# A two-layer attention trunk: where the second layer's gate is summed, and when the first layer's h is transposed

## The chip, the cores and the metric

The kernel runs on one core of a Trainium2 chip. Its time is the device time of one execution in microseconds (us), the median of several executions. The core's engines each work through their own queue in order: TensorE (PE, matmuls and transposes), VectorE (DVE), ScalarE (ACT), GpSimd (POOL) and SyncE (SP, which issues most of the DMAs). They wait for each other by semaphores.

## The reference

Two layers, each with 256 tokens of width 1024, all in float32:

```
mod = silu(c) @ w_ada + b_ada                 # w_ada: 1024 x 3072 per layer
shift, scale, gate = split(mod, 3)
h   = rms_norm(x, norm_g) * (1 + scale) + shift
z   = h @ w_in        # [c_q | c_kv | k_rope | g_mla | q | k | v | g_moba]
o_A = MLA causal attention (8 heads)     o_B = block-sparse causal attention (8 heads)
y   = concat(silu(g_mla) * o_A, silu(g_moba) * o_B) @ w_out
x   = x + gate * y
```

`c` is one row, so `mod` is a product of a vector and a matrix: 3072 columns for each layer, of which shift, scale and gate have 1024 each. The gate is needed only at the end of its layer, where it multiplies y; shift and scale are needed at its start.

## The kernel before

Everything is unrolled once by a planner inside the program (`Clock`). Coroutines for loads, splits, attention and so on wait in a heap by planned times; TensorE's large products are "units" that `run` takes in a written order, and between two units it lets every coroutine go whose planned time has come. What a coroutine issues stands in its engine's queue from then on, in that order. `charge` adds planned costs, `idle` holds back an instruction while its engine's planned queue is full, and `warm` puts dummy products of the identity (tile `idle`) in where TensorE is planned to stand still for more than `GAP` (2 us); `DENSE` sets how many.

**Products.** A weight (`raw_*`) comes by DMA in pieces of 256 rows; ScalarE mostly makes its rounded fp32r half (`whi_*`) and VectorE the rest (`wlo_*`, `split_lo`). h has halves `h_hi` and `h_lo` too, and each product is three matmuls (`mm3`): hi by hi, hi by lo, lo by hi. z goes by groups: `za` (latents and rotary key), `zga` and `zgb` (gates of the heads), `zbq`, `zbk`, `zbv`; `q` and `kv` come from the latents, `s`, `ptr` and `oT` are attention, `y` the output product. `URGENT` says how near to its use a split is no longer held back by `idle`.

**Modulation.** `w_ada` is read through 5 buffers (`ada`), each two k-tiles of 128 rows by 512 columns. `on_tensor` visits a block of 512 columns once all 8 k-tiles are there: `groups_sum` multiplies each k-tile by `crep` (silu(c) repeated 32 times), in TensorE's 32-column form, four k-tiles at once in four groups of 32 output rows. A block of shift or scale is then copied to `ev`, transposed and added up (`ss_sums`). A block of the gate is copied to `evg` (`gate_rows`) and a product with `rowsel` adds up its four rows and spreads the sum to all partitions (`gate_sums`); VectorE adds `b_ada`. `on_vector` is the other way, not used before: VectorE multiplies a k-tile by silu(c) of its rows and adds it to `acc`, k after k, and a product with `ones` adds up the partitions.

`modulation(l)` covers the gate of layer l and, in layer 0, shift and scale of layer 1. Before, all goes `on_tensor`: eight visits of 512 columns, first both gate blocks of layer 0, then layer 1's four blocks of shift and scale, then both gate blocks of layer 1. `ada_loader` loads in the same order, and all loads share SP's queue with the weights. `PERIOD` holds the planned distance of pieces on VectorE, a delay, and the planned distance of pieces on TensorE.

**h.** Layer 0's shift and scale are summed in five rounds (`sum_first`), as `w_ada` comes in. `h_T` transposes the normalised x (`xr`) on TensorE into `htr`, multiplies by scale and adds shift there (`ss`), and makes `h_hi` and `h_lo`. It waits for `ss` before it issues the transposes. At the layer boundary the second token tile's x (t = 1) comes from the last `y`, and TensorE goes through `za` of the first tile, some `zbq` of the first tile, and then `za` of the second.

Of the kernel before, what the change touches and what calls it, by code (L numbers as in the profile page):

```python
# [23 lines left out]
DEPTH = 2  # L24
# [10 lines left out]
PS = 4  # L35
MARGIN = 0.0
GAP = 2.0
DENSE = 0.6
BQ_FIRST = 2
ON = ("T", "T")  # L40
EARLY = True
FIRST = 0
TOGETHER = 9
VISIT = 8
WAIT = 0.25
# [8 lines left out]
LAG = 3  # L54
AHEAD = 4
SLACK = 0.35
URGENT = 2
BIAS = 0.7
WARM = 7
D_LAT = 0.95  # L60
D_0 = 4.0
HALVES = 12
DUMMY = 12
PERIOD = ((4.0, 0.0, 7.0), (8.0, 0, 20.0))
C_A, W_A = 0, 416
C_GA, C_QB, C_KB, C_VB, C_GB = 416, 928, 1440, 1952, 2464

# [7 lines left out]
class Clock:  # L75
# [34 lines left out]
    def give(self, tag, n=1):  # L110
        self.free[tag].extend([self.end + self.LAT] * n)

    def take(self, tag, n=1, spare=0):
        f = self.free[tag]
        while len(f) < n + spare:
            yield lambda: len(f) >= n + spare
        f.sort()
        t = f[n - 1]
        del f[:n]
        yield t  # L120

    def until(self, *keys):
        if not all(k in self.done for k in keys):
            yield lambda: all(k in self.done for k in keys)
        yield max(self.done[k] for k in keys)
# [7 lines left out]
    def start(self, gen, at=None):  # L133
        self.push(self.end if at is None else at, gen)
# [73 lines left out]
    def warm(self, t):  # L208

        if self.dummy and t - self.t["T"] > GAP:  # L210
            self.now, self.end, self.engine = self.t["T"], self.t["T"], None
            self.dummy(int((t - self.t["T"]) * DENSE / 0.11))

# [58 lines left out]
def trunk(ctx, tc, x, c, positions, norm_g, w_ada, b_ada, w_in, mla_q_norm_g, mla_w_uq,  # L272
# [10 lines left out]
    clk = Clock()  # L283
    V, A, T = Metered(nc.vector, "V", clk), Metered(nc.scalar, "A", clk), Metered(nc.tensor, "T", clk)
    P, G = Metered(nc.gpsimd, "P", clk), nc.gpsimd
    done, take, give, until, start, run = clk.done, clk.take, clk.give, clk.until, clk.start, clk.run

    def bank(name):
        return pp.tile([128, 512], F32, tag="ps", bufs=8, name=name)
# [48 lines left out]
    ones = cp.tile([128, 128], F32, name="ones")  # L338
# [65 lines left out]
    vec_a = cp.tile([128, N_A], F32, name="vec_a")  # L404
# [148 lines left out]
    def splitter():  # L553
        for i, (key, a, src) in enumerate(pieces):
# [4 lines left out]
            yield from take("w")  # L559
            urgent = lambda: i <= used[0] + URGENT  # L560
            raw, tag = halves[key, a]
# [68 lines left out]
    def ss_finish(l, w, ks, p_):  # L630

        n = len(ks)
        o = ss[l][:, w * 8 + ks[0]:w * 8 + ks[0] + n]
        b0 = V_B + 16 * l + w * 8 + ks[0]
        V.tensor_tensor(o, p_, vec_a[:, b0:b0 + n], op=ALU.add)
        if w == 1:
            V.scalar_tensor_tensor(o, o, 1.0, vec_a[:, V_NG + 8 * l + ks[0]:V_NG + 8 * l + ks[0] + n],
                                   op0=ALU.add, op1=ALU.mult)
        clk.mark(*(("ss", l, w, k) for k in ks))
# [27 lines left out]
    def on_vector(todo, begin, period):  # L667

        for i, ((m, w, j), k) in enumerate(todo):
            yield begin + i * period  # L670
            c0 = w * D + j * 512
            yield from until(("ada", m, c0, k))
            if k == 0:
                yield from take("acc")
                acc = acc_tile(f"acc{m}{j}")
            for n in range(2):
                yield from clk.idle("V")
                s_ = ada[m, c0, k][:, n]
                if k + n == 0:
                    V.tensor_scalar(acc, s_, cs[:, 0:1], None, op0=ALU.mult)  # L680
                else:
                    V.scalar_tensor_tensor(acc, s_, cs[:, k + n:k + n + 1], acc, op0=ALU.mult, op1=ALU.add)
                clk.engine = None
            give("ada")
            if k == KT - 2:
                yield
                start(gate_sums(m, j, acc, ones), clk.now)

    def gate_rows(l, j, p_):
        yield from take("acc")  # L690
# [6 lines left out]
    def gate_sums(l, j, acc, sel_):  # L697

        yield from take("ps")
        p_ = bank(f"ada{l}2{j}")  # L700
        T.matmul(p_, lhsT=sel_, rhs=acc, start=True, stop=True)
        give("acc")
        yield
        yield from until(("bg", l))
        g_ = gate[l][:, j * 512:j * 512 + 512]
        V.tensor_tensor(g_, p_, g_, op=ALU.add)
        give("ps")
        clk.mark(("gate", l, 2 * j), ("gate", l, 2 * j + 1))
# [7 lines left out]
    ada = {}  # L716

    def modulation(l, period):

        by_k = lambda blocks: [(b, k) for b in blocks for k in range(0, KT, 2)]  # L720
        gates_ = by_k((l, 2, j) for j in range(2))
        next_ = by_k((l + 1, w, j) for j in range(2) for w in (1, 0)) if l + 1 < DEPTH else []
        start(ada_loader(l, (gates_ + next_)))
        if ON[l] == "V":
            yield clk.now + period[1]
            start(on_vector(gates_, clk.now, period[0]), clk.now)
        start(on_tensor((gates_ if ON[l] == "T" else []) + next_, clk.now + period[1], period[2]), clk.now)
        yield from take("gate")
        gate[l] = cp.tile([128, D], F32, tag="gate", bufs=1, name=f"gate{l}")
        load(gate[l], bass.AP(tensor=b_ada.tensor, offset=b_ada[l, 2 * D:].offset, ap=[[0, 128], [1, D]]), ("bg", l))  # L730

    def on_tensor(todo, begin, period):

        for i, ((m, w, j), k) in enumerate(todo):
            if (k + 2) % VISIT:
                continue
            c0 = w * D + j * 512
            ks = range(k + 2 - VISIT, k + 2, 2)
            yield from until(*(("ada", m, c0, b) for b in ks))
            if k + 2 == VISIT:  # L740
                yield from take("ps", spare=1)
                p_ = bank(f"ada{m}{w}{j}")
            key = ("visit", m, w, j, k)

            def emit():
                groups_sum(p_, [ada[m, c0, b][:, n] for b in ks for n in range(2)], ks[0])
                give("ada", len(ks))
                clk.mark(key)
            clk.offer(max(clk.now, done["ada", m, c0, k] + ADA_LAG), emit, begin + i * period)
            yield from until(key)  # L750
            if k == KT - 2:
                start(gate_rows(m, j, p_) if w == 2 else ss_sums(m, w, tuple(range(4 * j, 4 * j + 4)), p_), clk.now)

    def ada_loader(l, todo):
        if l:
            yield from until(("loaded", l - 1))
        for (m, w, j), k in todo:
            yield from load_ada(m, w * D + j * 512, k)
        clk.mark(("loaded", l))
# [23 lines left out]
    def h_T(xr, l, groups):  # L783

        ps_ = []
        if l or not FIRST:
            yield from until(*(("ss", l, w, k) for w in (1, 0) for ks, _ in groups for k in ks))
# [692 lines left out]
    for l in range(DEPTH):  # L1480
        L = Ls[l]
        if l == 0 or not EARLY:
            start(modulation(l, PERIOD[l]))
        todo = names[l]
        if l == 1:
            first = L.proj(todo[0])
            second, m = L.proj(todo[1]), 2 * BQ_FIRST
# [5 lines left out]
        for name in todo:  # L1493
            run(L.gates(name) if name in ("ga", "gb") else mix(L.proj(name)))
        if l == 0 and EARLY:
            start(modulation(1, PERIOD[1]))
# [42 lines left out]
```

## Time and profile before

| | |
|---|---|
| time, median of 3 executions | 310.87 us (310.55 to 311.05) |
| profiled execution, its own time | 309.71 us |
| its span, first to last instruction | 307.6 us |
| TensorE busy | 296.6 us (96%) |
| VectorE busy | 217.0 us (71%) |
| ScalarE busy | 211.0 us (69%) |
| TensorE's mean granted clock | 0.992 |
| DMA | 65.20 MB, mean 212 GB/s |

Matmuls overlap in the array, so a row's duration is longer than the distance to the next row's start; that distance is what a matmul costs. In a timeline a row ends with the idle time ahead of it and what ended it, in brackets. All vector, scalar and tensor instructions have the line of the helper that records them (L230), so they are told apart by their tiles.

### The profile page before, as it was taken

How to read it: one execution, taken by the hardware profiler on the slowest of the kernel's cores; microseconds unless marked ns; L12 is line 12 of the kernel's file. 1: busy time of each engine (PE TensorE's matmuls, PEld its weight loads, DVE VectorE, ACT ScalarE, POOL GpSimd, SP SyncE). 2: the span in 40 equal slices, each digit the busy share in tenths (PEclk: the TensorE clock that was granted, in tenths of full speed). 3: DMA queues.
4: the chain of work that ended last, by engine and by line, in shares of the span. 5: the costliest groups of instructions: out<-in, count | busy, mean ns of one | idle time of the engine just before them, and what ended most of it. 6: DMA issues, size and time to landing. Idle time of an engine off the chain costs nothing.

```text
span 307.6 us, 5595 instructions
## 1 busy us (share of the span) xinstructions
PE 296.6 (96%) x1976; PEld 234.7 (76%) x1976; DVE 217.0 (71%) x635; ACT 211.0 (69%) x516; POOL 13.6 (4%) x40
## 2 busy tenths in 40 slices
PE   6989999999999899999999998999999999999995
PEld 5757779986668588665775968879999778777884
DVE  1344798664997979784876778699877598857544
ACT  5443367796695886986678896877587959685710
POOL 8700000000010000000000000000000000000000
PEclk9799999999999999999999999999999999999998
DMA  7999996895979975781843976665606450621012
GB/s 237 315 351 355 362 372 193 275 389 204 359 212 376 329 256 172 255 286 25 320 120 122 336 258 215 200 168 175 205 12 208 128 174 32 207 78 57 3 65 71
DMA packets 40299, 65.20 MB, mean 212 GB/s; under 512 B 2685, under 2 KB 16325, under 8 KB 40272
## 3 DMA queue, kind: packets, MB, share of 16 engines
q1 hardware_dynamic: 39360, 63.71, 62.5%
q0 software_dynamic: 816, 1.12, 1.4%
q8 instruction: 15, 0.25, 0.3%
q14 instruction: 12, 0.10, 0.1%
q10 hardware_dynamic: 96, 0.02, 0.0%
HBM read 63.79 MB, written 1.06 MB: 211 GB/s over the span
## 4 chain that ended last, share of the span: by engine, by line
PE 81%; DVE 7%; DMA 5%; ACT 5%; issue 1%; SPq 0%
PE y L230 15%; PE zbv L230 7%; PE ada L230 7%; PE zgb L230 7%; PE zga L230 7%; PE zbq L230 6%; PE zbk L230 6%; PE s L230 6%; PE za L230 4%; PE oT L230 4%; DMA raw_bv<-in_w_in_dram 3%; PE ptr L230 3%; PE q L230 2%; PE qtr L230 2%; DMA ada<-in_w_ada_dram 2%; PE warm L230 1%
## 5 line engine op out<-in xcount | busy, mean ns | idle before, releaser
L230 ACT ACTIVATE P<-P,sm 128x128 f32<-128x128 f32 (+1 forms) x116 | 47.8, 446 | 6.7 <-DVE sm L230 6.6
L230 PE MATMUL ada<-ada,crep 128*32 128x512 f32 (+2 forms) x272 | 25.2, 471 | 1.5 <-DMA ada<-in_w_ada_dram 1.5
L230 PE MATMUL y<-whi_o,gm 128*128 128x512 f32 (+1 forms) x72 | 23.8, 386 | 0.5 <-DVE gm L230 0.5
L230 DVE TENSOR_TENSOR wlo_o<-raw_o,whi_o 128x1024 fp32r<-128x1024 f32 x16 | 19.5, 1222 | 3.8 <-ACT whi_o L230 3.8
L230 PE MATMUL zga<-h_hi,whi_ga 128*128 128x256 f32 x64 | 19.3, 302 | 0.0
L230 PE MATMUL zgb<-h_hi,whi_gb 128*128 128x256 f32 x64 | 19.2, 300 | 0.0
L230 PE MATMUL zga<-h_hi,wlo_ga 128*128 128x256 f32 x64 | 18.2, 285 | 0.7 <-DVE wlo_ga L230 0.7
L230 PE MATMUL zgb<-h_hi,wlo_gb 128*128 128x256 f32 x64 | 18.1, 283 | 0.0
L230 PE MATMUL zga<-h_lo,whi_ga 128*128 128x256 f32 x64 | 18.1, 283 | 0.0
L230 PE MATMUL zgb<-h_lo,whi_gb 128*128 128x256 f32 x64 | 18.1, 283 | 0.0
L230 ACT CAST whi_o<-raw_o 128x1024 fp32r<-128x1024 f32 x15 | 15.6, 1044 | 1.6 <-PE y L230 1.6
L230 PEld LDWEIGHTS y<-whi_o,gm 128*128 128x128 f32 x72 | 13.1, 189 | 3.4 <-DVE gm L230 0.9
L230 PE MATMUL ptr<-ident,P 128*128 128x128 f32 x96 | 15.6, 273 | 0.0
L230 ACT ACTIVATE htr<-htr,ss 128x128 f32<-128x128 f32 (+1 forms) x21 | 9.7, 473 | 8.4 <-PE htr L230 5.0
L230 PEld LDWEIGHTS ptr<-ident,P 128*128 128x128 f32 x96 | 12.1, 140 | 4.4 <-DVE sm L230 0.8
L230 PEld LDWEIGHTS ada<-ada,crep 128*32 128x32 f32 x272 | 6.4, 110 | 11.4 <-issue 8.8
L230 PE MATMUL y<-whi_o,ga_hi 128*128 128x512 f32 (+1 forms) x36 | 15.0, 417 | 0.0
L230 PE MATMUL zbv<-whi_bv,h_hi 128*128 128x512 f32 x32 | 14.3, 446 | 0.0
L230 DVE CUSTOM_DVE_ANT_0 P<-s,bt 128x128 f32<-128x128 f32 (+1 forms) x32 | 9.5, 354 | 6.7 <-PE s L230 6.6
L230 PE MATMUL y<-whi_o,ga_lo 128*128 128x512 f32 (+1 forms) x36 | 13.4, 373 | 0.5 <-DVE ga_lo L230 0.5
L230 PE MATMUL zbk<-whi_bk,h_hi 128*128 128x512 f32 x32 | 13.8, 431 | 0.0
L230 PEld LDWEIGHTS zgb<-h_hi,whi_gb 128*128 128x128 f32 x64 | 12.2, 191 | 2.1 <-issue 2.1
(336 smaller groups left out, 878.5 us busy)
## 6 DMA issues: line engine op xcount, KB each, us to landing
ada<-in_w_ada_dram SPq DMA_DIRECT2D x44, 512.0 KB, 7.8
raw_o<-in_w_out_dram SPq DMA_DIRECT2D x16, 512.0 KB, 3.7
raw_ga<-in_w_in_dram SPq DMA_DIRECT2D x8, 512.0 KB, 6.0
raw_gb<-in_w_in_dram SPq DMA_DIRECT2D x8, 512.0 KB, 6.1
raw_bq<-in_w_in_dram SPq DMA_DIRECT2D x8, 512.0 KB, 3.9
raw_bk<-in_w_in_dram SPq DMA_DIRECT2D x8, 512.0 KB, 4.5
raw_bv<-in_w_in_dram SPq DMA_DIRECT2D x8, 512.0 KB, 4.7
raw_a<-in_w_in_dram SPq DMA_DIRECT2D x8, 416.0 KB, 6.1
```

The lines of the kernel that those rows point to most:

```text
L230: r = f(*args, **kw)
```

## The change

Layer 1's gate goes to VectorE (`ON`), and the blocks of layer 0's stage are visited in another order: gate block 0, scale and shift of layer 1's first half, gate block 1, scale and shift of its second half (`ORDER`), with 6 instead of 7 us planned between pieces. `modulation(1)` starts at the head of layer 1 rather than ahead of layer 0's output product (`EARLY`). `FIRST = 8` lets layer 0's transposes be issued before `ss` is there: only the step that multiplies waits for it. Half as many dummies are put into a planned gap (`DENSE`), and splits are urgent only one piece ahead (`URGENT`). `acc_sums` would sum shift or scale from VectorE's accumulator; with these settings nothing calls it.

```diff
--- before.py
+++ after.py
@@ -35,11 +35,12 @@
 PS = 4
 MARGIN = 0.0
 GAP = 2.0
-DENSE = 0.6
+DENSE = 0.3
 BQ_FIRST = 2
-ON = ("T", "T")
-EARLY = True
-FIRST = 0
+ON = ('TTTTTT', 'VV')
+EARLY = False
+ORDER = (4, 0, 1, 5, 2, 3)
+FIRST = 8
 TOGETHER = 9
 VISIT = 8
 WAIT = 0.25
@@ -54,14 +55,14 @@
 LAG = 3
 AHEAD = 4
 SLACK = 0.35
-URGENT = 2
+URGENT = 1
 BIAS = 0.7
 WARM = 7
 D_LAT = 0.95
 D_0 = 4.0
 HALVES = 12
 DUMMY = 12
-PERIOD = ((4.0, 0.0, 7.0), (8.0, 0, 20.0))
+PERIOD = ((4.0, 0.0, 6.0), (10.0, 0, 20.0))
 C_A, W_A = 0, 416
 C_GA, C_QB, C_KB, C_VB, C_GB = 416, 928, 1440, 1952, 2464
 
@@ -684,7 +685,20 @@
             give("ada")
             if k == KT - 2:
                 yield
-                start(gate_sums(m, j, acc, ones), clk.now)
+                start(gate_sums(m, j, acc, ones) if w == 2 else
+                      acc_sums(m, w, tuple(range(4 * j, 4 * j + 4)), acc), clk.now)
+
+    def acc_sums(l, w, ks, acc):
+
+        yield from until("vec_a")
+        yield from take("ps")
+        p_ = bank(f"ada{l}{w}{ks[0]}")
+        for b in range(4):
+            T.matmul(p_[:, b:b + 1], lhsT=acc[:, b * 128:b * 128 + 128], rhs=ones[:, 0:1], start=True, stop=True)
+        give("acc")
+        yield
+        ss_finish(l, w, ks, p_[:, 0:4])
+        give("ps")
 
     def gate_rows(l, j, p_):
         yield from take("acc")
@@ -718,13 +732,14 @@
     def modulation(l, period):
 
         by_k = lambda blocks: [(b, k) for b in blocks for k in range(0, KT, 2)]
-        gates_ = by_k((l, 2, j) for j in range(2))
-        next_ = by_k((l + 1, w, j) for j in range(2) for w in (1, 0)) if l + 1 < DEPTH else []
-        start(ada_loader(l, (gates_ + next_)))
-        if ON[l] == "V":
-            yield clk.now + period[1]
-            start(on_vector(gates_, clk.now, period[0]), clk.now)
-        start(on_tensor((gates_ if ON[l] == "T" else []) + next_, clk.now + period[1], period[2]), clk.now)
+        blocks = [(l, 2, j) for j in range(2)]
+        if l + 1 < DEPTH:
+            n_ = [(l + 1, w, j) for j in range(2) for w in (1, 0)]
+            blocks = [(n_ + blocks)[i] for i in ORDER]
+        of = lambda e: by_k(b for b, on in zip(blocks, ON[l]) if on == e)
+        start(ada_loader(l, by_k(blocks)))
+        start(on_vector(of("V"), clk.now, period[0]), clk.now)
+        start(on_tensor(of("T"), clk.now + period[1], period[2]), clk.now)
         yield from take("gate")
         gate[l] = cp.tile([128, D], F32, tag="gate", bufs=1, name=f"gate{l}")
         load(gate[l], bass.AP(tensor=b_ada.tensor, offset=b_ada[l, 2 * D:].offset, ap=[[0, 128], [1, D]]), ("bg", l))
```

TensorE's queue at the layer boundary, from the end of `za` of the first token tile on, before (`ada_2144` is gate block 0 of layer 1, `htr` are the transposes of the second tile's x):

```order
L230 MATMUL za_2150<-wlo_a_3_2061,h_hi 128x416
L230 MATMUL za_2150<-whi_a_3_2060,h_lo 128x416
L230 MATMUL ada_2144<-ada_2048_0_1841,crep 32x512 x2
L230 MATMUL ada_2144<-ada_2048_2_2062,crep 32x512 x2
L230 MATMUL ada_2144<-ada_2048_4_2064,crep 32x512 x2
L230 MATMUL ada_2144<-ada_2048_6_2066,crep 32x512 x2
L230 MATMUL htr_2225<-ident,xr_2012 128x128 x2
L230 MATMUL htr_2228<-ident,xr_2012 128x128 x2
L230 MATMUL zbq_2231<-whi_bq_0_2136,h_hi 128x512
L230 MATMUL zbq_2231<-wlo_bq_0_2137,h_hi 128x512
L230 MATMUL zbq_2231<-whi_bq_0_2136,h_lo 128x512
L230 MATMUL htr_2243<-ident,xr_2012 128x128 x2
```

The same place now:

```order
L231 MATMUL za_2160<-whi_a_3_2105,h_lo 128x416
L231 MATMUL htr_2203<-ident,xr_2042 128x128 x2
L231 MATMUL htr_2206<-ident,xr_2042 128x128 x2
L231 MATMUL htr_2223<-ident,xr_2042 128x128 x2
L231 MATMUL htr_2226<-ident,xr_2042 128x128 x2
L231 MATMUL zbq_2237<-whi_bq_0_2164,h_hi 128x512
L231 MATMUL zbq_2237<-wlo_bq_0_2165,h_hi 128x512
L231 MATMUL zbq_2237<-whi_bq_0_2164,h_lo 128x512
L231 MATMUL zbq_2237<-whi_bq_0_2164,h_hi 128x512
L231 MATMUL zbq_2237<-wlo_bq_0_2165,h_hi 128x512
L231 MATMUL zbq_2237<-whi_bq_0_2164,h_lo 128x512
L231 MATMUL idle<-ident 128x128 x6
```

The visit of the gate block is gone, the transposes of all four groups stand directly behind `za`, and behind two units of `zbq` six dummies have come in.

VectorE's queue from the second tile's `h_lo` on, before:

```order
L230 TENSOR_TENSOR gate_2180<-ada_2275,gate_2180 128x512
L230 TENSOR_TENSOR h_lo<-htr_2225,h_hi 128x2x128
L230 TENSOR_TENSOR h_lo<-htr_2243,h_hi 128x2x128
L230 TENSOR_TENSOR h_lo<-htr_2228,h_hi 128x2x128
L230 TENSOR_TENSOR h_lo<-htr_2249,h_hi 128x2x128
L230 SCALAR_TENSOR_TENSOR cT1vb<-ctr_2288,vec,cT1cT 128x128 x3
L230 TENSOR_TENSOR wlo_uq_1_2312<-raw_uq_1_2223,whi_uq_1_2311 128x2x384
L230 TENSOR_TENSOR wlo_ukv_0_2322<-raw_ukv_0_2247,whi_ukv_0_2321 128x1024
L230 TENSOR_TENSOR wlo_bq_2_2345<-raw_bq_2_2280,whi_bq_2_2344 128x1024
```

And now (`acc_2181` is the sum of gate block 0, `ada_2048_0` its first two k-tiles):

```order
L231 TENSOR_TENSOR h_lo<-htr_2203,h_hi 128x2x128
L231 TENSOR_TENSOR h_lo<-htr_2223,h_hi 128x2x128
L231 TENSOR_TENSOR h_lo<-htr_2206,h_hi 128x2x128
L231 TENSOR_TENSOR h_lo<-htr_2226,h_hi 128x2x128
L231 TENSOR_SCALAR acc_2181<-ada_2048_0_2137,cs 128x512
L231 SCALAR_TENSOR_TENSOR acc_2181<-ada_2048_0_2137,cs,acc_2181 128x512
L231 TENSOR_TENSOR wlo_uq_0_2277<-raw_uq_0_2194,whi_uq_0_2276 128x2x384
L231 SCALAR_TENSOR_TENSOR cT1vb<-ctr_2282,vec,cT1cT 128x128 x3
L231 TENSOR_TENSOR wlo_uq_1_2307<-raw_uq_1_2235,whi_uq_1_2306 128x2x384
L231 SCALAR_TENSOR_TENSOR acc_2181<-ada_2048_2_2139,cs,acc_2181 128x512
L231 TENSOR_TENSOR wlo_ukv_0_2319<-raw_ukv_0_2261,whi_ukv_0_2318 128x1024
L231 SCALAR_TENSOR_TENSOR acc_2181<-ada_2048_2_2139,cs,acc_2181 128x512
```

Sums over the gate's k-tiles now stand between the splits of `uq` and `ukv`; two more stand ahead of the next split of `zbq`, the last two of the block much later, and the eight of block 1 by the splits of `zbk`.

TensorE's queue in `zga` of layer 1, before (`ada_2297` is gate block 1):

```order
L230 MATMUL zga_2500<-h_hi,wlo_ga_0_2421 128x256
L230 MATMUL ada_2297<-ada_2560_0_2070,crep 32x512 x2
L230 MATMUL ada_2297<-ada_2560_2_2235,crep 32x512 x2
L230 MATMUL ada_2297<-ada_2560_4_2237,crep 32x512 x2
L230 MATMUL ada_2297<-ada_2560_6_2239,crep 32x512 x2
L230 MATMUL qtr_2530<-ident,kn_2352 96x128 x4
L230 MATMUL zga_2538<-h_hi,whi_ga_0_2420 128x256
L230 MATMUL zga_2538<-h_lo,whi_ga_0_2420 128x256
L230 MATMUL zga_2538<-h_hi,wlo_ga_0_2421 128x256
```

And now, at the same place:

```order
L231 MATMUL zga_2494<-h_hi,wlo_ga_0_2438 128x256
L231 MATMUL zga_2494<-h_hi,whi_ga_0_2437 128x256
L231 MATMUL zga_2494<-h_lo,whi_ga_0_2437 128x256
L231 MATMUL zga_2494<-h_hi,wlo_ga_0_2438 128x256
L231 MATMUL zga_2507<-h_hi,whi_ga_0_2437 128x256
L231 MATMUL zga_2507<-h_lo,whi_ga_0_2437 128x256
L231 MATMUL zga_2507<-h_hi,wlo_ga_0_2438 128x256
L231 MATMUL zga_2507<-h_hi,whi_ga_0_2437 128x256
L231 MATMUL zga_2507<-h_lo,whi_ga_0_2437 128x256
L231 MATMUL zga_2507<-h_hi,wlo_ga_0_2438 128x256
```

The visit is gone, and the products with `rowsel` too. A product with `ones`, one for each block, stands at the head of `zgb` and in `zbk` instead.

## Rows read from the trace of the kernel before

**Rows 1.** The page, busy time of each engine.

```profile
PE 296.6 (96%) x1976; PEld 234.7 (76%) x1976; DVE 217.0 (71%) x635; ACT 211.0 (69%) x516; POOL 13.6 (4%) x40
```

**Rows 2.** Windows: length, busy us of PE, PEld, DVE, ACT, POOL, PEclk, DMA, GB/s.

```profile
184.75:202.50 17.75, 16.80 (x83) 14.79 (x83) 14.02 (x35) 13.54 (x34) 0.00 (x0) 1.00 0.64 204
```

**Rows 3.** Timeline, TensorE, layer boundary: start, duration, instruction.

```profile
177.18 0.35 PE L230 MATMUL za<-wlo_a,h_hi 128*128 128x416 f32 x1
177.36 0.35 PE L230 MATMUL za<-whi_a,h_lo 128*128 128x416 f32 x1
177.65 1.92 PE L230 MATMUL ada<-ada,crep 128*32 128x512 f32 x16
179.50 0.66 PE L230 MATMUL htr<-ident,xr 128*128 128x128 f32 x4
...
181.82 1.02 PE L230 MATMUL ada<-evg,rowsel 128*128 128x512 f32 x2
...
184.59 0.35 PE L230 MATMUL za<-wlo_a,h_hi 128*128 128x416 f32 x1
185.89 0.46 PE L230 MATMUL za<-whi_a,h_lo 128*128 128x416 f32 x1 [0.95 <-DVE h_lo L230]
```

**Rows 4.** Timeline, TensorE, zga of layer 1.

```profile
202.43 0.28 PE L230 MATMUL zga<-h_hi,wlo_ga 128*128 128x256 f32 x1
...
202.79 0.28 PE L230 MATMUL zga<-h_hi,wlo_ga 128*128 128x256 f32 x1
202.99 1.92 PE L230 MATMUL ada<-ada,crep 128*32 128x512 f32 x16
204.85 0.64 PE L230 MATMUL qtr<-ident,kn 128*96 128x128 f32 x4
```

**Rows 5.** Timeline, ScalarE, layer boundary.

```profile
177.46 0.72 ACT L230 ACTIVATE xr<-xs,rx 128x512 f32<-128x512 f32 x1 [0.31 <-DVE rx L230]
...
180.00 0.57 ACT L230 COPY evg<-ada 128x512 f32<-128x512 f32 x1
```

**Rows 6.** Timeline, VectorE, layer boundary and start of layer 1.

```profile
184.16 0.68 DVE L230 TENSOR_TENSOR gate<-ada,gate 128x512 f32<-128x512 f32 x1
184.75 1.41 DVE L230 TENSOR_TENSOR h_lo<-htr,h_hi 128x256 fp32r<-128x256 f32 x4
...
198.23 1.22 DVE L230 TENSOR_TENSOR wlo_ga<-raw_ga,whi_ga 128x1024 fp32r<-128x1024 f32 x1
...
210.39 1.22 DVE L230 TENSOR_TENSOR wlo_gb<-raw_gb,whi_gb 128x1024 fp32r<-128x1024 f32 x1
```

**Rows 7.** Instructions on tile ada: count, duration min/median/max.

```profile
L230 DVE SCALAR_TENSOR_TENSOR acc<-ada,cs,acc x7: 474/480/485, 39.3 to 44.1; 128x256 f32<-128x256 f32 x7
```

**Rows 8.** Groups by form, VectorE: count, busy us, mean ns of one.

```profile
L230 DVE TENSOR_TENSOR h_lo<-htr,h_hi 128x256 fp32r<-128x256 f32 x10 | 3.8, 418 | 1.7 <-ACT h_hi L230 1.7
...
L230 DVE TENSOR_TENSOR h_lo<-htr,h_hi 128x512 fp32r<-128x512 f32 x3 | 2.1, 691 | 1.3 <-ACT h_hi L230 1.2
...
L230 DVE TENSOR_SCALAR xr<-xs,rx 128x512 f32<-128x512 f32 x2 | 1.0, 487 | 0.1
```

**Rows 9.** Timeline, TensorE, first use of zgb's split.

```profile
224.62 0.28 PE L230 MATMUL zgb<-h_hi,wlo_gb 128*128 128x256 f32 x1
```

**Rows 10.** Timeline, TensorE, end of layer 0.

```profile
169.09 0.50 PE L230 MATMUL y<-whi_o,gm 128*128 128x512 f32 x1 [0.46 <-DVE gm L230]
```

**Rows 11.** Timeline, TensorE, first layer.

```profile
14.21 0.44 PE L230 MATMUL htr<-ident,xr 128*128 128x128 f32 x2
...
15.68 0.46 PE L230 MATMUL za<-whi_a,h_hi 128*128 128x416 f32 x1 [0.23 <-ACT h_hi L230]
...
19.77 0.38 PE L230 MATMUL zga<-h_hi,wlo_ga 128*128 128x256 f32 x1 [0.75 <-DVE wlo_ga L230]
```

**Rows 12.** Timeline, VectorE, first layer: shift and scale of round 0.

```profile
13.53 0.16 DVE L230 SCALAR_TENSOR_TENSOR ss<-ss,vec_a 128x1 f32<-128x1 f32 x1
```

**Rows 13.** Windows, as rows 2, first layer.

```profile
4.00:12.00 8.00, 6.55 (x53) 4.63 (x53) 2.21 (x9) 4.72 (x13) 6.20 (x15) 0.81 1.12 321
```

## The prediction, made before the result was known

> **What bounds the kernel now.** I read the page first, then TensorE's timeline stage by stage, then the queues of the engines it waits for. TensorE is busy 96% of the span, VectorE 71% [rows 1]. In the timeline a matmul costs the distance to the next start, and nearly everywhere from 20 us on those distances are even: TensorE works through a queue without waiting. The places where it does wait are few and short: for VectorE's `h_lo` at the layer boundary [rows 3], for `gm` at the end of layer 0 [rows 10], for the first split of `zga` [rows 11]. So time is gained by taking work out of TensorE's queue, if nothing comes in its place, and lost wherever VectorE hands over a split or `h_lo` later than TensorE now asks for it.
>
> **The visits that go.** Layer 1's two gate visits leave TensorE. One runs from 177.65 to the next start at 179.50, 1.85 us; `za` products follow each other by 0.18 us (177.18, 177.36), but the visit starts 0.29 behind the last, so entering it costs 0.10 more [rows 3]. The other is 202.99 to 204.85, and enters late by about 0.08 [rows 4]. That is 2 x 1.95 = 3.9 us. The product that adds up the partitions stays (`ones` for `rowsel`) and moves: the pair at 181.82 is busy 1.02 us [rows 3], of which I count 0.9. One such product leaves the layer boundary, and one more than before stands behind it. The copies to `evg` leave ScalarE and are needed no more.
>
> **What the boundary gives back.** The first visit stood where TensorE has little else to do. It restarts `za` of the second tile at 185.89; its last product before that started at 184.59, so 1.1 us were spent waiting for `h_lo` [rows 3]. Without the visit and the `rowsel` product TensorE would be there 1.95 + 0.9 = 2.85 us earlier and wait up to 2.85 + 1.1 us, unless `h_lo` comes earlier too. It does: ScalarE's half of x was done at 177.46 + 0.72 = 178.18 [rows 5], but the transposes stood behind the visit until 179.50, 1.3 us; the copy to `evg` (0.57) stood in ScalarE's queue ahead of the work on them [rows 5], and the 0.68 us of adding the gate directly ahead of the first `h_lo` [rows 6]. All but the ScalarE copy depend on what else is in the queues then (`cn` and the splits of `zbq`), so `h_lo` is earlier by 0.6 us (the copy alone) to 2.0 (transposes and gate). I take 1.4, between the ends since both the copy and the gate go for certain. TensorE restarts 1.4 earlier. Behind it the second visit goes (1.95) and a `ones` product comes (0.9). Together -1.4 - 1.95 + 0.9 = -2.45 us. The six dummies behind `zbq` lie in that wait. Four transposes of the same width are busy 0.66 us [rows 3], so six products of two records each take at most 2.0; they cost nothing while the wait is longer than they are, and up to 2.0 if there were none.
>
> **What VectorE takes on.** 16 sums of 128x512: two that begin a block, like the 0.487 us of the scaled x, and 14 with an accumulator. The trace shows these at 128x256 with 0.480 us [rows 7]; 256 more columns cost 0.691 - 0.418 = 0.27 in another two-input operation [rows 8], so 0.75 us. That is 2 x 0.49 + 14 x 0.75 = 11.5 us, on an engine that is off the path only while its splits are early. They are early by 13 us at `zgb` (split from 210.39 to 211.61, first used at 224.62) [rows 6, 9], so the second block and two sums of the first cost nothing there. They are not early at the head of layer 1. From the first `h_lo` at 184.75 to the end of `zga`'s first split at 198.23 + 1.22 = 199.45 [rows 6] are 14.7 us, in which VectorE stands still 3.7 us (17.75 - 14.02 in a stretch that it otherwise fills) [rows 2], so it works 11.0. The order now puts six sums in (0.49 + 5 x 0.75 = 4.2), and moves in a split of `uq`, three products for `cT1vb` and a reduction, some 2.8 us. That makes 18.0 us if it never stands still, 21.7 if it stands still as long as before. TensorE asks for the split 202.43 - 184.75 = 17.7 us behind that `h_lo` [rows 4, 6]. The wait is 0.3 to 4.0 us; it can't be a gain, since no split comes sooner. I take 0.8, near the low end: the sums need only data that has long landed, so they run where VectorE now waits for ScalarE.
>
> **Behind the sums in other queues.** An `ada` buffer is freed only when VectorE has summed it, and SP issues in order: the loads of gate block 1 wait there, and the weights of `zga` queue behind them. That is in the slower rival below.
>
> **End of layer 0.** The last visit of scale and shift moves forward out of the last `y` products, and its reduction out of VectorE's queue ahead of `gm`; the wait of 0.46 us at 169.09 [rows 10] should go. I count 0.4 (0 to 0.46, and up to 0.9 lost if the reordered attention opens a wait like the boundary's).
>
> **First layer.** `ss` of round 0 is ready at 13.53 + 0.16 = 13.69 [rows 12], the transposes start only at 14.21, and the first `za` at 15.68 [rows 11]. With the transposes done beforehand, `za` can be some 0.5 to 0.9 us earlier. But the queue then stands at 19.77 for `zga`'s split [rows 11], which follows its own weight and ScalarE's copy of round 1's sums. I take a third, 0.3 (0 to 0.9; the six dummies put in ahead of `zga` could cost up to 2.0).
>
> **Sum.** -2.45 + 0.8 - 0.4 - 0.3 = -2.35, rounded to -2.4 us. On the profiled execution (309.71, span 307.6 and 2.1 around it) that is 307.3. It lay 1.2 below the median of 310.87, which is the number to compare with: 308.5 us.
>
> **Rivals.** *All of it is kept* (0.20): `h_lo` 2.0 earlier, VectorE's sums wholly hidden, first layer 0.9: -2.0 - 1.95 + 0.9 - 0.46 - 0.9 = -4.4, 306.5 us. For it: VectorE's idle time at the head of layer 1 is nearly as long as the sums. Against: every split there would have to be just in time. *Nothing is left* (0.10): `h_lo` only 0.6 earlier, 1.5 us of wait for the splits, no gain elsewhere: -0.6 - 1.95 + 0.9 + 1.5 = -0.15, 310.7 us. *VectorE becomes the bound at the head of layer 1* (0.16): the sums stand in its queue ahead of the splits of `ukv`, `zbq` and `zga`, its waits for ScalarE remain, and the loads of gate block 1 hold back the weights of `zga` at SP. The wait is then the full 4.0 us: -2.45 + 4.0 = +1.55, 312.4 us. It decides from a wait of 2.45 us on. For it: the stretch has only 3.7 us to spare for 7 us of added work; against: the splits behind `zga`'s first are early. *The clock falls at the boundary* (0.04): TensorE's granted clock is 1.00 (2.4 GHz) over the stretch that begins with its wait of 1.1 us [rows 2, 3], but 0.81 over 4 to 12 us, where it first stood idle for data and was then at 1.2 GHz for a part of the stretch [rows 13], a loss of 0.19 x 8.0 = 1.5 us. If a wait of two to four us brought the same, -2.4 + 1.5 = -0.9, 310.0 us. The Trainium skill (TensorE: Matmul & The Clock Gate, section HAM oscillation — how this bites in real kernels) says that waits for data in the middle of a kernel let the clock fall to half; no wait of this trace from 20 us on shows it, and the six dummies stand in this one.
>
> **How the numbers follow.** The forecast, -1.2 to -3.6 us (307.3 to 309.7), gets 0.50, the rivals 0.20, 0.10, 0.16 and 0.04. A measurement of this kernel can tell 0.2%, 0.6 us, from no change. Faster by more: 0.50 + 0.20 + part of the last, 0.72. Within: 0.11. Slower: 0.17. The range reaches from the low rival to half-way into the slow one: 306.2 to 311.6.
>
> **What would show it.** Right: in the profile after, no 32-column product behind layer 0, the transposes at the boundary right behind `za`, a wait for `h_lo` of about 2 to 2.5 us there (dummies included), and a wait of under 2 us in all for the splits of `ukv`, `zbq` and `zga`. From `zga`'s second piece on TensorE should run without waits and stay 2 to 3 us ahead. Wrong: waits for splits of over 2.5 us, a granted clock below 1.00 past 20 us, new waits in layer 0's attention, or a boundary without a wait.

## The result, and the profile after

The changed kernel takes 308.88 us, median of 10 runs (308.06 to 310.12), against 310.93 of the kernel before on the same chip (10 runs, 309.54 to 313.11): -2.05 us, ratio 0.9938 with a 95% interval of 0.9911 to 0.9965, that is -2.8 to -1.1 us. The forecast was 308.5 us, in a range of 306.2 to 311.6.

The executions of either kernel lie in an early and a late group (the changed kernel's five at 308.06 to 308.64 and five at 309.11 to 310.12, the kernel before's two at 309.54 and 309.93 and eight from 310.55 on); by the groups' medians the change is -1.45 (from two runs of the kernel before) and -1.16, and the rest of the 2.05 would be that more of the changed kernel's runs were early. The two profiled executions, on which the stretches below are read, took 308.32 and 309.71, -1.4 us.

The page's line of busy times, against [rows 1]:

```profile
PE 295.4 (96%) x1966; PEld 235.4 (77%) x1966; DVE 220.7 (72%) x642; ACT 215.4 (70%) x523; POOL 13.6 (4%) x40
```

TensorE's 3.7 us of visits are gone, but 12 dummies (2.5 us in two groups) came, so its busy time fell by 1.2 only. Where the 1.4 us come from is read with one call for both kernels: TensorE's windows, cut at the same five events (last `zgb` of layer 0, first `za` of layer 1, first `zga` of layer 1, last `zgb`, last `y`). The columns are start and end, length, busy time, granted clock, DMA share, GB/s. Before:

```profile
0.00:62.49 62.49, 57.89 (x468) 0.97 0.96 308
62.49:173.07 110.58, 108.76 (x664) 1.00 0.72 249
173.07:202.19 29.12, 28.17 (x147) 1.00 0.70 229
202.19:237.49 35.30, 35.30 (x285) 1.00 0.51 146
237.49:303.72 66.23, 66.23 (x419) 1.00 0.28 94
```

After:

```profile
0.00:61.98 61.98, 57.82 (x479) 1.00 0.98 312
61.98:171.96 109.98, 108.89 (x665) 1.00 0.67 226
171.96:200.44 28.48, 27.24 (x142) 1.00 0.89 305
200.44:235.04 34.60, 33.83 (x269) 1.00 0.49 137
235.04:302.37 67.33, 67.33 (x420) 1.00 0.32 106
```

The start gave 0.51, the rest of layer 0 0.60, the boundary and the head of layer 1 0.64, `zga` and `zgb` 0.70; the last stretch takes 1.10 more. Layer 1 as a whole, the part that lost 3.7 us of visits, is only 0.24 us shorter. (The start is no measure of the change: executions of the same program differ there by up to 2 us, as the end of the part on the prediction shows.)

The boundary after, on TensorE (columns as in [rows 3]):

```profile
176.78 1.06 PE L231 MATMUL htr<-ident,xr 128*128 128x128 f32 x8
...
179.09 1.50 PE L231 MATMUL idle<-ident 128*128 128x128 f32 x12
...
181.76 0.50 PE L231 MATMUL zbq<-wlo_bq,h_hi 128*128 128x512 f32 x1 [0.94 <-DVE wlo_bq L231]
...
183.43 0.59 PE L231 MATMUL ctr<-ident,cn 128*128 128x128 f32 x3 [0.26 <-ACT cn L231]
183.79 0.43 PE L231 MATMUL za<-whi_a,h_hi 128*128 128x416 f32 x1
184.05 0.35 PE L231 MATMUL za<-wlo_a,h_hi 128*128 128x416 f32 x1
184.24 0.35 PE L231 MATMUL za<-whi_a,h_lo 128*128 128x416 f32 x1
```

The transposes stand right behind `za`, as forecast, and TensorE no longer waits for `h_lo` (184.05 to 184.24 is an even step). It waits earlier, for the split of `zbq`'s second piece. Why that is late, VectorE's queue shows:

```profile
180.16 0.42 DVE L231 TENSOR_SCALAR htr<-htr,ss 128x128 f32<-128x128 f32 x1 [1.53 <-ACT htr L231]
180.49 1.22 DVE L231 TENSOR_TENSOR wlo_bq<-raw_bq,whi_bq 128x1024 fp32r<-128x1024 f32 x1
...
182.62 1.41 DVE L231 TENSOR_TENSOR h_lo<-htr,h_hi 128x256 fp32r<-128x256 f32 x4
```

The split waits in order behind a modulation of h, and that for ScalarE's part (1.53 us). ScalarE in turn does the sums of `cn` first:

```profile
177.71 0.38 ACT L231 ACTIVATE cn<-za 128x256 f32<-128x256 f32 x1
...
178.91 1.23 ACT L231 ACTIVATE htr<-htr,ss 128x128 f32<-128x128 f32 x3
```

So the transposes came 2.7 us earlier (179.50 [rows 3] to 176.78), but `cn` follows the end of `za`, which came only 0.8 earlier, and ScalarE's order made the modulation follow `cn`.

VectorE from the first `h_lo` to `zga`'s second split, and what TensorE then met; last the `ones` product and the product behind it:

```profile
182.60:201.30 18.70, 17.98 (x89) 15.40 (x87) 17.13 (x39) 14.54 (x40) 0.00 (x0) 1.00 0.79 254
```

```profile
201.32 0.39 PE L231 MATMUL zga<-h_hi,wlo_ga 128*128 128x256 f32 x1 [0.48 <-DVE wlo_ga L231]
...
220.52 1.02 PE L231 MATMUL ada<-acc,ones 128*128 128x512 f32 x2
220.98 0.68 PE L231 MATMUL zgb<-h_hi,whi_gb 128*128 128x256 f32 x1
221.50 0.28 PE L231 MATMUL zgb<-h_lo,whi_gb 128*128 128x256 f32 x1
```

The window's row gives length and busy time of PE, PEld, DVE, ACT and POOL in turn: VectorE is busy in 17.1 of 18.7 us. The wait for `zga`'s first split is 0.48 us; f1 below shows that the sums are not its cause. The `ones` product takes 0.46 to the next start, and that next one 0.52 instead of 0.12: 0.86 in all.

### The profile page after: what moved, and what is told of

The parts are those of the page before. It is cut to its first block, busy times and chain, and to the rows that moved or that the text cites. A ratio compares the mean times of both kernels' runs of the same rounds, so it can differ in the third digit from the quotient of the medians.

```text
span 306.3 us, 5579 instructions
## 1 busy us (share of the span) xinstructions
PE 295.4 (96%) x1966; PEld 235.4 (77%) x1966; DVE 220.7 (72%) x642; ACT 215.4 (70%) x523; POOL 13.6 (4%) x40
## 3 DMA queue, kind: packets, MB, share of 16 engines
q0 software_dynamic: 816, 1.12, 1.5%
## 4 chain that ended last, share of the span: by engine, by line
PE 70%; DVE 10%; DMA 8%; ACT 7%; SPq 2%; issue 2%; DVEq 0%
PE y L231 13%; PE zgb L231 8%; PE zbv L231 7%; PE zga L231 7%; PE ada L231 6%; PE zbk L231 5%; PE s L231 5%; PE oT L231 4%; PE ptr L231 3%; DMA ada<-in_w_ada_dram 3%; PE za L231 3%; PE zbq L231 3%; SPq L514 2%; DMA raw_bv<-in_w_in_dram 2%; DMA raw_bq<-in_w_in_dram 2%
## 5 line engine op out<-in xcount | busy, mean ns | idle before, releaser
L231 PE MATMUL ada<-ada,crep 128*32 128x512 f32 (+2 forms) x240 | 21.3, 445 | 2.3 <-DMA ada<-in_w_ada_dram 2.2
L231 PE MATMUL zgb<-h_hi,whi_gb 128*128 128x256 f32 x64 | 19.9, 310 | 0.3 <-DVE sm L231 0.3
L231 ACT COPY PT<-ptr 128x512 f32<-128x512 f32 (+1 forms) x23 | 11.1, 481 | 8.5 <-PE ptr L231 8.4
L231 ACT CAST whi_o<-raw_o 128x1024 fp32r<-128x1024 f32 x16 | 16.6, 1048 | 0.0
L231 DVE SCALAR_TENSOR_TENSOR acc<-ada,cs,acc 128x512 f32<-128x512 f32 (+1 forms) x21 | 13.9, 660 | 0.4
L231 ACT COPY ev<-ada 128x512 f32<-128x512 f32 (+1 forms) x9 | 4.6, 513 | 13.1 <-PE ada L231 13.1
```

The source lines that it names most:

```text
L231: r = f(*args, **kw)
```

## Experiments

Two kinds. Where a setting of the kernel is changed, its planner lays everything out anew (so in the kernels e1 to e8). In f1 to f3, g1 and g2 the planner was charged as in the changed kernel, so that every other instruction of every engine keeps its place. Ratios are against the kernel before, run beside each on the same chip. Against the changed kernel's 0.9938 they tell apart about 1.1 us (both half-widths together, 0.0035); a trace tells a few tenths of a stretch.

**f1: the sums left out, order kept.**

```diff
                 else:
-                    V.scalar_tensor_tensor(acc, s_, cs[:, k + n:k + n + 1], acc, op0=ALU.mult, op1=ALU.add)
+                    a_ = acc, s_, cs[:, k + n:k + n + 1], acc
+                    clk.charge("V", V._cost("scalar_tensor_tensor", acc, a_, {}))
```

> The changed kernel with 14 of the 16 sums left out of VectorE's queue and every other instruction of every engine in the same order (the gate is therefore not the reference's). Theory A (the sums' price is the waits of zga and zgb for their splits, 0.5 + 0.4 us): 308.0 us (307.6 to 308.4), TensorE starts zga's first split without a wait and the boundary's wait of 0.94 us for zbq's second piece stays, since no sum stands ahead of it. Theory B (VectorE's sums also hold back ScalarE and the attention of layer 1): 307 us or less. Theory C (they cost nothing): 308.9 us within 0.3.

309.27 us, ratio 0.9939 (0.9914 to 0.9964), as the changed kernel. Layer 1 in the three windows above:

```profile
173.61:202.12 28.51, 27.26 (x142) 1.00 0.89 308
202.12:236.30 34.18, 33.85 (x268) 1.00 0.48 136
236.30:303.63 67.33, 67.33 (x420) 1.00 0.33 106
```

Only the middle one is shorter, by 0.42 us, and that is the wait for `zga`'s split. But this is not what the sums cost. e3 below has all the sums, in the same order in layer 1, and its profiled execution has no such wait either; its middle window:

```profile
201.55:235.75 34.20, 33.84 (x269) 1.00 0.49 136
```

g1 and f3, with the sums too, take 34.21 and 34.20. What was late in the changed kernel's execution is a weight: ScalarE's `whi_bq` waited for it to land, what follows on ScalarE came 0.4 us later, and VectorE waits for ScalarE's `sk` ahead of `zga`'s split. First the changed kernel, then the same cast in e3, without a wait:

```profile
191.78 1.05 ACT L231 CAST whi_bq<-raw_bq 128x1024 fp32r<-128x1024 f32 x1 [0.30 <-DMA raw_bq<-in_w_in_dram]
195.35 0.42 DVE L231 COPY va<-kv 128x256 f32<-128x256 f32 x1 [1.26 <-ACT sk L231]
```

```profile
192.46 1.06 ACT L231 CAST whi_bq<-raw_bq 128x1024 fp32r<-128x1024 f32 x1
```

(In g2 the weight was late too, by 0.22, and the wait for `zga`'s split is 0.37.) Without the sums VectorE stands still in their place; f1 has here

```profile
194.10 1.23 DVE L231 TENSOR_TENSOR wlo_bq<-raw_bq,whi_bq 128x1024 fp32r<-128x1024 f32 x1 [0.93 <-ACT whi_bq L231]
```

So the sums cost nothing that these traces resolve (34.18 without them, 34.20 with): C, and A and B are out. Whether the sums have a part in the late landing, through the `ada` buffers that they hold, is not shown; it is there in two of five executions with the sums once and in this order.

**f2: the sums done twice, order kept.**

```diff
+                    V._engine.scalar_tensor_tensor(acc, s_, cs[:, k + n:k + n + 1], acc, op0=ALU.mult, op1=ALU.add)
```

> The changed kernel with 14 of the 16 sums executed twice, every other instruction in the same order (the gate is not the reference's): 10.4 us more on VectorE, 3.75 to 4.5 of them between the first h_lo of layer 1 and zga's first split. Theory A (VectorE is just at its limit there: it works 17.1 of 18.7 us, and the split ends 0.06 us ahead of its use): TensorE waits 2.2 to 4 us more ahead of zga, 311.1 to 313 us. Theory B (VectorE's order leaves room, since its waits for ScalarE shrink instead): under 309.9 us.

314.48 us, ratio 1.0109 (1.0074 to 1.0144). The two largest of TensorE's waits from 176 to 260 us (in total, times, longest):

```profile
PE zbq L231 <- DVE wlo_bq L231: 1.5, 2, 1.0
PE kv L231 <- DVE wlo_ukv L231: 1.3, 1, 1.3
```

Layer 1 takes 135.42 us instead of 130.41: 10.4 us more work on VectorE make it 5.0 us longer, 2.8 of them ahead of `zga`. A, and more than A behind it. With the sums twice VectorE is the bound from there on; the sums once still fit.

**g1: a visit in the place of the boundary's dummies, order kept.**

```diff
-                T.matmul(p_[:, 0:128], lhsT=ident, rhs=ident, start=True, stop=True)
+                if clk.t["T"] < 100:
+                    T.matmul(p_[:, 0:128], lhsT=ident, rhs=ident, start=True, stop=True)
+                else:
+                    clk.charge("T", T._cost("matmul", p_[:, 0:128], (), dict(lhsT=ident)))
+            if clk.t["T"] > 100:
+                groups_sum(p_, [halves[("bq", 1), 0][0][:, i % 2].bitcast(F32) for i in range(KT)], 0)
```

> The changed kernel with a whole visit (8 products of 32 columns by 512, their result unused) in the place of the six dummies at the boundary between the layers, every other instruction in the same order. Theory A (the boundary is bound by the chain from the last y over x, its transposes and their modulation to h_lo and wlo_bq, so a visit there costs nothing, and taking it away gave nothing): the visit of 1.95 us fills the 1.25 us of the dummies and 0.7 of the 0.94 us of wait behind them; the wait shrinks to about 0.3 us, za of the second tile starts within 0.2 us as before, 308.9 us within 0.5. Theory B (the visit is worth what the prediction counted, 1.4 of 2.85 us with its ones product): 309.6 us or more, za of the second tile starts 0.7 us later or more.

309.51 us, ratio 0.9950 (0.9926 to 0.9975); layer 1 takes 130.07 us. TensorE:

```profile
179.25 1.92 PE L647 MATMUL idle<-whi_bq,crep 128*32 128x512 f32 x16
181.10 0.50 PE L231 MATMUL zbq<-whi_bq,h_hi 128*128 128x512 f32 x1
181.82 0.51 PE L231 MATMUL zbq<-wlo_bq,h_hi 128*128 128x512 f32 x1 [0.23 <-DVE wlo_bq L231]
```

The wait shrinks from 0.94 to 0.23 and the split's product starts at 181.82 instead of 181.76. A: a visit here is free. (The 0.34 us by which layer 1 is shorter are the wait ahead of `zga`'s split, which this execution does not have.)

**g2: a visit in `zga`, order kept** (the same eight products behind `zga`'s first unit).

```diff
+                run(us[:1])
+                p_ = bank("visit")
+                groups_sum(p_, [halves[("ga", 1), 0][0][:, i % 2].bitcast(F32) for i in range(KT)], 0)
+                us = us[1:]
```

> The changed kernel with a whole visit (8 products of 32 columns by 512, their result unused) put into zga of layer 1 behind its first unit, near where the second visit stood before, every other instruction in the same order. Theory A (there TensorE has nothing to wait for, a visit costs its 1.95 us): 310.4 us (310.1 to 310.9), less 0.5 if the wait for zga's first split goes into it; the lead does not come back later. Theory B (VectorE is so near its limit that the later splits only wait for less): 309.4 us or less, the waits of zga and zgb for splits (0.5 and 0.4 us) gone and the order of the attention behind it unchanged.

311.03 us, ratio 1.0029 (1.0002 to 1.0055). The window from `zga` to the last `zgb` grows from 34.60 to 36.69, the one behind it stays (67.34). A: here a visit costs all of its time, 2.1 us.

**f3: no dummies, order kept.**

```diff
-                T.matmul(p_[:, 0:128], lhsT=ident, rhs=ident, start=True, stop=True)
+                clk.charge("T", T._cost("matmul", p_[:, 0:128], (), dict(lhsT=ident)))
```

> The changed kernel without its two groups of six dummies (1.25 us each, at 16.6 and 179.1 us), every other instruction in the same order. Theory A (they lie in waits that end when data comes): 308.9 us within 0.3; TensorE's wait for zbq's second split becomes 2.2 us instead of 0.94, and the granted clock stays 1.00 there. Theory B (the dummies stand in TensorE's way, since behind them it waits for something that starts only after them): 1.2 to 2.5 us faster. Theory C (without them the wait is long enough for the clock to fall): a granted clock under 1.00 behind 182 us and 0.6 us or more slower.

311.2 us, ratio 0.9997 (0.9968 to 1.0026): some 1.8 us lost. The boundary, and TensorE's windows behind it:

```profile
186.81 0.50 PE L231 MATMUL zbq<-wlo_bq,h_hi 128*128 128x512 f32 x1 [2.29 <-DVE wlo_bq L231]
```

```profile
184.00:188.00 4.00, 1.71 (x8) 0.97 0.95 330
188.00:192.00 4.00, 4.00 (x16) 0.60 0.49 137
```

The wait is 2.29, as A has it, but behind it TensorE's granted clock is 0.60: it stood at 1.2 GHz for a part of these 4 us, and `za` takes 1.0 us longer in all. The same happens behind the gaps that the first group left (waits of 0.49 and 0.75 us, then 0.83 over 20 to 30 us, against 1.00). The profiled execution took 314.2 us, the longest of twelve, so the loss is read from the ratio and not from it; the lower clock is in all of them: their mean granted clock is 0.975 to 0.993, that of the changed kernel's ten 0.992 to 1.00 and of f1's nine 0.989 to 1.00. C: the dummies are worth more than they cost.

**e5: splits urgent two pieces ahead.**

```diff
-URGENT = 1
+URGENT = 2
```

> The changed kernel with splits urgent two pieces ahead instead of one, so that at the boundary wlo_bq's second piece stands ahead of the modulation of h on VectorE. Theory A (the wait of 0.94 us for that split is a cost of its own): 308.0 us (307.6 to 308.4). Theory B (the chain to cn and h_lo sets the restart, the wait only moves to them): 308.9 us within 0.4, with a wait of about 1 us or more at ctr or za instead of zbq. Theory C (a wait of over 2 us at the boundary with no dummies in it lets the granted clock fall): a clock below 1.00 in the four microseconds behind it, 310 us or more.

311.85 us, ratio 1.0033 (1.0008 to 1.0058).

```profile
184.51 0.71 PE L231 MATMUL ctr<-ident,cn 128*128 128x128 f32 x3 [2.62 <-ACT cn L231]
```

```profile
184.00:188.00 4.00, 3.20 (x12) 0.78 0.22 83
188.00:192.00 4.00, 4.00 (x19) 0.80 0.69 188
```

No wait for `wlo_bq`, but all of it at `ctr`, with no dummies in it, and the clock falls again: B for the place, C for the clock. The price is not C's alone: of the 3 us over the changed kernel layer 1 has 1.0 (131.43 us against 130.41), and 1.8 lie in layer 0 (111.79 against 109.98 from the last `zgb` to layer 1), which the planner laid out anew.

**e2: the gate alone, in the kernel before.**

```diff
-ON = ("T", "T")
-EARLY = True
+ON = ("T", "V")
+EARLY = False
...
-PERIOD = ((4.0, 0.0, 7.0), (8.0, 0, 20.0))
+PERIOD = ((4.0, 0.0, 7.0), (10.0, 0, 20.0))
```

> The kernel before with only the gate of layer 1 summed up on VectorE (same sums, begun at the start of layer 1); order of blocks, modulated transposes, dummies and urgency stay as before. Theory A (the gate move is worth the 1.65 us of the prediction's sum): 0.5% under the kernel before, about 309.3 us. Theory B (the gate move is worth the 5.4 us that putting it back cost): 1.7% under, 305.6 us. Theory C (the boundary wait that remains and the splits give it all back, the gain of the whole change is that of its other parts): within 0.5 us of the kernel before.

310.64 us, ratio 1.0006 (0.9982 to 1.0029): C. Layer 1 takes 130.32 us against 130.65. The place of the first visit is an open wait:

```profile
184.23 0.72 PE L230 MATMUL ctr<-ident,cn 128*128 128x128 f32 x3 [2.60 <-ACT cn L230]
```

In this execution the clock stayed at 1.00, so a wait of 2.6 us need not bring it down.

**e1: the gate back on TensorE, in the changed kernel.**

```diff
-ON = ('TTTTTT', 'VV')
-EARLY = False
+ON = ('TTTTTT', 'TT')
+EARLY = True
```

> The changed kernel with only the gate of layer 1 put back on TensorE (four visits' worth of 32-column products, started before layer 0's output projection as in the kernel before); unmodulated transposes, order of blocks, dummies and urgency stay as changed. Theory A (the visits are what was gained): -2.45 at the boundary and +0.8 of waits for splits come back with the opposite sign, +1.65 us over the changed kernel's 308.9, 310.5 us (310.0 to 311.0); the boundary shows a wait of about 1 us for h_lo again, and layer 1 from zga on is 1.5 to 2.5 us later. Theory B (VectorE's sums give the visits back, the gain is that of layer 0's order and of the first layer, za of layer 1 starting 1.1 us earlier): 308.9 us within 0.5.

(It is two visits, not four as the text on record says.) 314.32 us, ratio 1.0107 (1.0085 to 1.0130), by the ratios some 5.3 over the changed kernel; neither theory. The planner did not put the visits back: one now stands in the last `y` of layer 0 (167.45), with its product over the partitions at 171.62, the other in the middle of `za` (178.89), none in a wait, and `ptr` waits 1.1 us for `qn` in layer 1. It prices visits where they are not hidden, not the change.

**e8: layer 0's blocks in the old order, at the old distance.**

```diff
-ORDER = (4, 0, 1, 5, 2, 3)
+ORDER = (4, 5, 0, 1, 2, 3)
...
-PERIOD = ((4.0, 0.0, 6.0), (10.0, 0, 20.0))
+PERIOD = ((4.0, 0.0, 7.0), (10.0, 0, 20.0))
```

> The changed kernel with the blocks of layer 0 (gate, scale and shift) in the order and at the period of the kernel before. Theory A (the order is worth the wait of 0.46 us for gm at the end of layer 0): 309.3 us (309.0 to 309.7), and the wait before a y product near 168 us is back. Theory B (the order of blocks gives the 0.6 us by which the stretch from the last zgb of layer 0 to the first za of layer 1 became shorter, or more): 309.5 to 310.5. Theory C (nothing): 308.9 us within 0.3.

311.69 us, ratio 1.0030 (1.0010 to 1.0051), 2.8 us over the changed kernel, more than any theory. From the last `zgb` to layer 1 it takes 111.75 us against 109.98; in the attention there stand

```profile
148.18 0.44 PE L231 MATMUL ptr<-ident,P 128*128 128x128 f32 x2 [0.70 <-DVE sm L231]
149.27 0.50 PE L231 MATMUL y<-whi_o,gm 128*128 128x512 f32 x1 [0.65 <-ACT gm L231]
```

The wait near 168 us is not back. Order matters more than the one wait that I priced.

**e3: the first layer's h transposed modulated.**

```diff
-FIRST = 8
+FIRST = 0
```

> The changed kernel with only the transposes of the first layer put back to modulated h (they wait for ss of the round). Theory A (the first layer is worth 0.3 us, since the queue stands anyway at zga's split and at the landing of the next round's ada block): 309.2 us (308.8 to 309.8), za of layer 1 starts at most 0.5 us later than the changed kernel's 171.96. Theory B (half of the gain is made here: the first za at 13.53 instead of 15.68 us): 310.0 us or more, za of layer 1 starts 1 us later or more.

309.41 us, ratio 0.9940 (0.9919 to 0.9962), as the changed kernel. `za` of layer 1 starts at 173.04, which reads as B; but f1, whose program is the changed kernel's up to there, starts it at 173.61, so this start says nothing. A by the time.

**e7: the sums begun behind the head of layer 1.**

```diff
-        if l == 0 or not EARLY:
+        if l == 0:
             start(modulation(l, PERIOD[l]))
...
             todo = todo[2:]
+            start(modulation(1, PERIOD[1]))
```

> The changed kernel with the gate's loads and sums begun only when the projections at the head of layer 1 are laid out (ahead of zga's units), so that no sum and no ada load stands ahead of the splits of uq, ukv, zbq and zga's first pieces; the kernel is the same up to the boundary. Theory A (the sums at the head cost 0.8 us): 308.1 us (307.6 to 308.6), if the splits of gb and bk, which stand 10 us ahead, take the sums without a wait. Theory B (sums at the head are free and late sums press the splits of zbk and zbv, where the changed kernel already loses 1.1 us): 309.5 us or more, with new waits of TensorE between 235 and 275 us.

310.05 us, ratio 0.9966 (0.9943 to 0.9988). The wait for `zga`'s split is gone, as it is with the sums in place in e3, f3 and g1, and 0.7 us of a wait of `s` for ScalarE's `sg` are new; layer 1 takes 130.64 us, in e3 130.04 and in g1 130.07. Nothing gained: B.

**e6: as f1, but laid out anew.**

```diff
+                if k + n:
+                    continue
                 s_ = ada[m, c0, k][:, n]
```

> The changed kernel with 14 of the 16 sums of layer 1's gate left out (only the first of each block is computed, so the gate is not the reference's; loads, ones products and the addition stay). Theory A (the sums cost 0.8 us at the head of layer 1 as waits of zbq and zga for their splits, and the 1.1 us that layer 1 loses from 237 us on is also VectorE's): 308.9 - 0.8 = 308.1 us or, with the later loss, 307.0; the waits of 1.1 us at zbq's second piece and 0.5 us at zga's first split shrink below 0.4 each. Theory B (VectorE has room, the sums lie where it waits for ScalarE, and these waits come from other work): 308.9 us within 0.3, waits as before.

310.7 us, ratio 0.9989 (0.9975 to 1.0004): slower than with the sums. Less work gave another order, with waits that the changed kernel does not have (0.32 us at `zbq`, 195.87, and 0.9 for `gm` in layer 0). f1 answers the question, this run does not.

No run was clearly faster than the changed kernel.

## Why the prediction was right, and where it was not

The time was right, and in part by luck. In the two profiled executions, where the sum can be checked stretch by stretch, the change is worth 1.4 us and not 2.4; the median's interval (-2.8 to -1.1) holds both, and that the median itself came out at -2.05, so near the forecast, is no proof of the sum. Of the terms, the boundary gave 0.64 us of the 1.4 forecast, layer 1 from `zga` on lost 0.40 where the sum has a gain of 0.25 (-1.95, +0.9, +0.8), and layer 0 gave 1.11 instead of 0.7.

- **Boundary, h_lo 1.4 us earlier and TensorE with it.** `h_lo` came 1.3 us earlier, counted from the end of `za` (177.36 to 184.75 [rows 3, 6], now 176.56 to 182.62). TensorE did not follow: from the first `za` to the first `zga` it gained 0.64. This is the step that failed. I let `h_lo` alone set the restart and left `cn` and the splits of `zbq` as something that `h_lo` depends on; they are waited for themselves, and end last once `h_lo` is early. The wait for `h_lo` of 2 to 2.5 us that was to show the prediction right did not come; it is one for `wlo_bq`. g1 and e2 show the other side: a visit in that wait is free, and where only the gate moved (e2) a wait of 2.60 us stands in the first visit's place, with the stretch to `zga` 0.41 shorter.
- **Second visit, -1.95.** g2 puts it at 2.1. The stretch that it stood in became only 0.70 shorter: 0.42 of the rest is the wait for `zga`'s split, which a late weight brought (f1), 0.28 a wait for `sm` in `zgb` that was not forecast. The others (0.7, by the 1.95 some 0.5) are open: the same products stand there in another order.
- **Ones product, +0.9.** 0.86. One of the two now stands behind `zgb`, and so the last stretch gives 1.1 us back. The remaining 0.2 are open.
- **VectorE's sums.** Their durations were right (0.745 us median, 0.75 forecast), and so was the 18.0 to 21.7 us from the first `h_lo` to the end of `zga`'s split: 182.62 to 201.26, 18.6. The price was not: 0.8 counted, nothing found (f1), since the wait that the trace shows is a late weight's. The ground that I gave for the low end, that the sums run where VectorE waits for ScalarE, is what f1 shows, and should have carried the term to nothing. That VectorE becomes the bound was a fair rival: f2 shows that twice the sums cost 5 us.
- **Waits for splits under 2 us in all.** 0.94 and 0.48, 1.4. But neither is the sums' doing: ahead of the 0.94 no sum stands and it stays in f1, and the 0.48 is the late weight's.
- **End of layer 0, -0.4.** The wait of [rows 10] is gone, and the stretch is 0.60 shorter. e8 shows that in the changed kernel the order of the blocks and their distance carry 1.8 us of this stretch, so the term was right in its sign and place but is not one wait: TensorE's waits here fell from 1.8 to 1.1 us, and all of the 1.1 are new (0.6 us of `s` for `bqT`, 0.5 for `PT`). New waits in layer 0's attention were a sign of being wrong; they came, but smaller than those that went.
- **First layer, -0.3.** Not resolved in the time (e3). In the trace the first `za` starts at 13.53 instead of 15.68, but by the last `zgb` 0.51 of 2.15 us is left: TensorE waits for the landing of an `ada` block (1.12 us, up to 20.37). The 0.51 itself is within what the start varies by.
- **The dummies lie in the wait.** Right, and more: without them f3 loses 1.8 us, and the clock falls. The rival of the falling clock was rated 0.04 on the ground that they stand there. It was a rule of the Trainium skill (TensorE: Matmul & The Clock Gate, section HAM oscillation — how this bites in real kernels) that waits for data let the clock fall; f3 and e5 agree (2.29 and 2.62 us, then 0.60 and 0.78), e2 does not (2.60 us, then 1.00).

Why executions of one program differ by more than a microsecond shows in their start. f1 and f2 have the changed kernel's program up to the boundary, but in their profiled executions `zgb` of layer 0 ended at 63.51 and 64.02 instead of 61.98. TensorE's windows of f1 there:

```profile
8.00:12.00 4.00, 4.00 (x33) 0.55 1.17 306
12.00:16.00 4.00, 4.00 (x26) 0.60 1.13 336
```

Over both the changed kernel had 1.00. In f2 the clock reads 1.00 too, but its products took as long as f1's, so the durations are the safer sign. Four products of the same dummies, in the changed kernel and in f1 (in f2 1.22):

```profile
9.24 0.71 PE L231 MATMUL warm<-ident 128*128 128x128 f32 x4
```

```profile
9.94 1.23 PE L231 MATMUL warm<-ident 128*128 128x128 f32 x4
```

The program is the same, so the layout of the kernel doesn't decide it alone. What does stays open; the first `ada` block landed later in f1 and f2 (TensorE waits 1.61 and 2.20 us for it, 1.07 in the changed kernel), which is no proof.

## What to carry to other kernels

Work that stands in a wait is worth nothing when it is taken away, and all of its time elsewhere: before counting it, list everything that TensorE waits for behind it, and take the latest, not the one that the profile names today. Where a planner lays out the kernel, an experiment that changes a setting changes the order everywhere, and the order alone moved the time by 1 to 3 us here; charge the planner as before and change one instruction. A wait that one trace shows need not be the change's: follow it to what ended it, and look for it in a second trace of the same queue, before it gets a price.

## What the hardware showed that I had not expected

Six small products in a wait of 2.2 us go with a clock that stays: 1.00 behind it in every profile that has them there (the changed kernel, e3, f1, f2, g2), 0.60 over 4 us in f3 without them; e2 kept 1.00 without any. The granted clock of a window can read 1.00 where the products are slow: in f2 over 8 to 16 us, where four `warm` products took 1.22 us, as against 1.23 in f1 at a clock of 0.55. The same instructions in the same order reached the end of layer 0's `zgb` at 61.98, 63.51 and 64.02 us in three profiled executions (the changed kernel, f1, f2), and layer 1's first `za` at 171.96, 173.61 and 173.74.
